# Loading and splitting the input projection's weights ahead of the modulation's weights

## The chip, the cores and the metric

The kernel runs on one core of one Trainium2 chip. The metric is the device time of one execution in microseconds. The core has a matrix engine (TensorE, PE in the profile; its weight loads are PEld), a vector engine (VectorE, DVE), an activation engine (ScalarE, ACT), a general engine (GpSimd, POOL), a queue engine that issues most of the transfers (SyncE, SP), and 16 DMA engines.

## The reference, cut to what matters

One transformer layer over 2048 latent tokens and 256 context tokens of width 1024, all in float32:

```
mod = silu(cond) @ w_ada + b_ada            # 1024 -> 6 x 1024: shift, scale, gate, shift, scale, gate
p   = (layer_norm(x) * (1 + scale) + shift) @ w_in    # 1024 -> 1184: 384 query, 256 key/value, 32 rope, 512 S5
```

`p` feeds a latent attention and a state-space (S5) mixer, whose outputs are projected, added and normalised, and a gated feed-forward block follows. The change touches only the start: the first two of the six parts of `mod` (shift and scale), for latent and context conditions, and the weights `w_in` of the input projection.

## The kernel before

Float32 products are made of three products of rounded halves. `hi_of` (line 53, on GpSimd) rounds a raw tile to its upper half, `lo_of` (line 58, on VectorE) subtracts that from the raw tile, and `mm3` (lines 63 to 65) multiplies high by high, high by low and low by high. The whole program is a chain of stages whose TensorE work is written out one behind the other; the stage around the change is `phase_in`, which takes about the first 390 us.

`phase_in` stages all its loads through one tag, `st`, of a pool with six buffers of 128x1024. In code order it issues:

1. the S5 tables' small loads (`s5_prep`, on ScalarE's queue) and their first transposes,
2. `load(0)`: two tiles of context tokens (`xt`, line 130), and their normalisation (lines 71 to 91 and 137). They keep two of the six buffers until `front(0)` has transposed them,
3. `wada`: sixteen tiles of 512 KB of `w_ada` (line 148), each of which TensorE multiplies by the two conditions straight from the buffer, with four matmul instructions in the trace (line 150), into four PSUM tiles `pa`,
4. `wraw`: sixteen tiles of 296 KB of `w_in` (line 159), each split by GpSimd into `wih` and by VectorE into `wil`, which stay for the whole stage,
5. `mrow`, `pm`, `mod`: the sums are copied (167), transposed (169) and biased (172, 173),
6. `front(0)`: the context tokens are transposed (191, `pt`), modulated (195, `ur`) and split into `uh` and `ul`,
7. the rest of the S5 tables' preparation: exponentials, sine and powers on VectorE (536 to 605), transposes on TensorE (636 `pbt`, 643 `pct`), and products on VectorE (657 to 662). Its scratch `sp_a` and `sp_b` lies in one of the two `uh` and one of the two `ul` buffers,
8. for each of nine groups of 256 tokens: `front` of the next group, `project` of this one (`pkv`, from the second group on `pq`, and `p` for the S5 part), and beside them pieces of two generators, `multiply` and `contract` of the S5 tables (681 to 714, GpSimd products, then `pin` on TensorE and stores from SP's queue) and `modulations` (309 to 323, the other four parts of `mod`, loaded by SP as `wad` and summed on VectorE).

A scheduler orders the instructions of each engine at build time by readiness and by code order. So an engine's order can differ from the code's (VectorE's exponentials of step 7 run in the first 30 us), and then it is fixed: each engine, SP's queue too, takes its instructions in that order. The PSUM tag `tr` has two buffers, which `pm`, `pt`, `pbt` and `pct` take in code order.

Of the kernel before, what the change touches and what calls it, by code (L numbers as in the profile page):

```python
# [10 lines left out]
F32 = mybir.dt.float32  # L11
# [39 lines left out]
def hi_of(eng, hi, raw):  # L51

    eng.tensor_scalar(hi, raw, 1.0, 0.0, ALU.mult, ALU.add)  # L53


def lo_of(eng, lo, raw, hi):

    eng.tensor_tensor(lo, raw, hi.bitcast(F32), ALU.subtract)  # L58
# [39 lines left out]
def phase_in(tc, E):  # L98
    nc = tc.nc
    I = E.I  # L100
    with ExitStack() as st:
        cp = st.enter_context(tc.tile_pool(name="in_c", bufs=1, reuse_waits="tile"))
        stage = st.enter_context(tc.tile_pool(name="in_stage", bufs=6, reuse_waits="tile"))
# [4 lines left out]
        ps_p = st.enter_context(tc.tile_pool(name="in_pp", bufs=1, space=PSUM, reuse_waits="tile"))  # L108
# [12 lines left out]
        cT = cp.tile([128, 32], F32, name="cT")  # L121
        nc.vector.tensor_copy(cT, pc[:, 0, 0:32])

        def load(gi):
            src = I["ctx"][0] if gi == 0 else I["x"][0]
            base = 0 if gi == 0 else (gi - 1) * 256
            xs = []
            for i in range(2):
                x = stage.tile([128, 1024], F32, name="xt", tag="st")
                nc.sync.dma_start(x, src[base + i * 128: base + (i + 1) * 128, :])  # L130
                xs.append(x)
            return xs

        def norm(xs):
            for x in xs:
                mv, rs = ln_stats(nc, sm, x, eps)
                nc.vector.tensor_scalar(x, x, mv[:, 0:1], rs, ALU.subtract, ALU.mult)
            return xs
# [2 lines left out]
        prep = s5_prep(tc, E, cp, tp, stage, up, ps_t, ps_p)  # L141
        next(prep)
        ns0 = norm(load(0))
        pa = [ps_p.tile([2, 512], F32, name="pa%d" % i, tag=t) for i, t in enumerate(("pq", "pkv0", "pkv1", "ps0"))]
        for k in range(8):
            for b in range(2):
                w = stage.tile([128, 1024], F32, name="wada", tag="st")
                nc.sync.dma_start(w, I["w_ada"][0, k * 128:(k + 1) * 128, b * 1024:(b + 1) * 1024])
                for hf in range(2):
                    nc.tensor.matmul(pa[b * 2 + hf], cT[:, k:16:8], w[:, hf * 512:(hf + 1) * 512],  # L150
                                     start=(k == 0), stop=(k == 7))

        whi, wlo = [], []
        for k in range(8):
            hi = wp.tile([128, 1184], F32R, name="wih%d" % k)
            lo = wp.tile([128, 1184], F32R, name="wil%d" % k)
            for o in (0, 592):
                raw = stage.tile([128, 1024], F32, name="wraw", tag="st")
                nc.sync.dma_start(raw[:, 0:592], I["w_in"][0, k * 128:(k + 1) * 128, o:o + 592])
                hi_of(nc.gpsimd, hi[:, o:o + 592], raw[:, 0:592])  # L160
                lo_of(nc.vector, lo[:, o:o + 592], raw[:, 0:592], hi[:, o:o + 592])
            whi.append(hi)
            wlo.append(lo)
        pm = ps_t.tile([128, 16, 2], F32, name="pm", tag="tr")
        for b in range(4):
            mrow = tp.tile([128, 2, 256], F32, name="mrow", tag="ur").rearrange("p a b -> p (a b)")[0:2]
# [1750 lines left out]
def build(tc, ins, out, dbg=None, phases="abcdefg"):  # L1917
# [4 lines left out]
    with ExitStack() as st:  # L1922
# [10 lines left out]
        if "a" in phases:  # L1933
            phase_in(tc, E)
# [72 lines left out]
```

## Time and profile before

| what | us |
|---|---|
| median of three runs | 3241.45 (3236.36 to 3243.56) |
| profiled execution, its own time | 3237.78 |
| its span | 3235.9 |
| TensorE busy | 3064.9 (95%) |
| VectorE, GpSimd, ScalarE busy | 2260.4, 1573.3, 1275.6 |
| DMA, mean over the span | 118 GB/s |

Busy shares are averages over stages with different limits. In a row of the timeline the first number is the start and the second the length in us, and the bracket at the end gives the idle time of the engine before it and what ended it. An engine's name with a q is its instruction queue.

### The profile page before, as it was taken

Reading aid. Unit: us, or ns where it says so; the run is one execution under the profiler, and the core shown is the slowest. Engines: PE = TensorE matmul, PEld = TensorE weight load, DVE = VectorE, ACT = ScalarE, POOL = GpSimd, SP = SyncE. Lnnn points to the kernel's source line nnn. Section 1 sums busy time; section 2 is a strip of 40 time slices with the busy share of each in tenths; the row PEclk is TensorE's granted clock in tenths of the full one; section 3 lists DMA queues with packets and bytes.
Section 4 is the critical chain, followed back from the end, with each engine's and each line's share of the span. In section 5 each row is a group of like instructions: output and inputs, shape, how many; then the busy total and the mean of one; then the engine's idle time right before and its main releaser. Section 6 shows DMA issues by size and latency. Waiting matters only on the chain. (4 is left out here: it accounts for less than half of the span.)

```text
span 3235.9 us, 48094 instructions
## 1 busy us (share of the span) xinstructions
PE 3064.9 (95%) x16693; PEld 2602.4 (80%) x16693; DVE 2260.4 (70%) x3906; ACT 1275.6 (39%) x2400; POOL 1573.3 (49%) x2365
## 2 busy tenths in 40 slices
PE   7899988999999999999888989999999999999998
PEld 3788876989889898889666767888688888888886
DVE  7755356888888776788568586766866666566667
ACT  2333354677777666677635232321300002112110
POOL 3755333777877899935234243332222222243345
PEclk9999999999999999999989999999999999999999
DMA  7454474011111122221677633332422224555544
GB/s 235 156 163 137 131 257 143 25 28 32 33 26 28 51 75 81 77 68 41 158 207 211 183 114 101 121 105 91 147 91 85 85 85 152 190 187 164 176 147 137
DMA packets 372565, 382.14 MB, mean 118 GB/s; under 512 B 97177, under 2 KB 270297, under 8 KB 372321
## 3 DMA queue, kind: packets, MB, share of 16 engines
q1 hardware_dynamic: 302320, 307.31, 31.9%
q10 hardware_dynamic: 70000, 71.75, 6.5%
q8 instruction: 132, 2.16, 0.3%
q14 instruction: 113, 0.92, 0.1%
HBM read 274.48 MB, written 104.48 MB: 117 GB/s over the span
## 5 line engine op out<-in xcount | busy, mean ns | idle before, releaser
L1033 DVE TENSOR_TENSOR ptl<-tps,pth 128x512 fp32r<-128x512 f32 x576 | 380.7, 685 | 99.4 <-ACT pth L1027 99.1
L1027 ACT CAST pth<-tps 128x512 fp32r<-128x512 f32 x576 | 336.0, 586 | 159.3 <-PE tps L1022 144.3
L53 POOL TENSOR_SCALAR gh<-wraw 128x512 fp32r<-128x512 f32 x220 | 179.8, 819 | 423.1 <-PE pc L64 75.3
L1045 PE MATMUL O<-pth,vhl 128*128 128x256 f32 x1152 | 323.3, 304 | 0.6 <-DVE oo L1054 0.6
L1046 PE MATMUL O<-ptl,vhl 128*128 128x256 f32 x1152 | 298.1, 283 | 2.0 <-DVE ptl L1033 1.9
L999 DVE TENSOR_REDUCE mx<-SB 128x1 f32<-128x1280 f32 x128 | 190.7, 1490 | 77.7 <-PE SB L65 77.7
L1046 PEld LDWEIGHTS O<-ptl,vhl 128*128 128x128 f32 x1152 | 219.5, 191 | 10.1 <-DVE ptl L1033 3.5
L1045 PEld LDWEIGHTS O<-pth,vhl 128*128 128x128 f32 x1152 | 218.0, 189 | 7.6 <-ACT pth L1027 1.1
L58 DVE TENSOR_TENSOR gl<-wraw,gh 128x512 fp32r<-128x512 f32 x216 | 166.0, 773 | 79.6 <-POOL gh L53 75.3
L1564 ACT CAST oh<-uraw 128x512 fp32r<-128x512 f32 x144 | 85.5, 620 | 308.5 <-PE pd L64 147.2
L1022 PE MATMUL tps<-ident,PB 128*128 128x128 f32 x1280 | 193.0, 273 | 3.2 <-DVE ptl L1033 3.2
L1010 ACT ACTIVATE PB<-SB,nm 128x1280 f32<-128x1280 f32 x128 | 170.7, 1334 | 4.6 <-DVE nm L1004 4.5
L1022 PEld LDWEIGHTS tps<-ident,PB 128*128 128x128 f32 x1280 | 152.6, 140 | 22.8 <-DVE ptl L1033 6.1
L999 DVE TENSOR_REDUCE mx<-SA 128x1 f32<-128x1024 f32 x128 | 156.0, 1219 | 17.3 <-PE SA L65 17.1
L1022 PE MATMUL tps<-ident,PA 128*128 128x128 f32 x1024 | 152.7, 274 | 1.6 <-DVE ptl L1033 1.6
L58 DVE TENSOR_TENSOR ol<-uraw,oh 128x512 fp32r<-128x512 f32 x136 | 104.6, 790 | 63.0 <-ACT oh L1564 62.8
L63 PE MATMUL SB<-kh,qh 96*128 96x512 f32 (+1 forms) x384 | 145.8, 380 | 0.0
L1010 ACT ACTIVATE PA<-SA,nm 128x1024 f32<-128x1024 f32 x128 | 143.4, 1121 | 5.2 <-DVE nm L1004 5.2
L774 POOL TENSOR_TENSOR sct<-scan_tab,hist 128x128 f32<-128x128 f32 x286 | 132.3, 463 | 24.5 <-ACT hist L763 4.9
L1692 ACT ACTIVATE s<-s 128x512 f32<-128x512 f32 x43 | 27.1, 631 | 286.1 <-DVE s L1691 286.0
L64 PE MATMUL SB<-kl,qh 96*128 96x512 f32 (+1 forms) x384 | 138.3, 360 | 0.0
L65 PE MATMUL SB<-kh,ql 96*128 96x512 f32 (+1 forms) x384 | 138.1, 360 | 0.0
(577 smaller groups left out, 9653.2 us busy)
## 6 DMA issues: line engine op xcount, KB each, us to landing
wraw<-in_w_down SPq DMA_DIRECT2D x198, 256.0 KB
wraw<-in_w_gate_up SPq DMA_DIRECT2D x176, 256.0 KB
h_scr<-s ACTq DMA_DIRECT2D x88, 256.0 KB
uraw<-h_scr SPq DMA_DIRECT2D x88, 256.0 KB
wad<-in_w_ada SPq DMA_DIRECT2D x32, 512.0 KB
wada<-in_w_ada SPq DMA_DIRECT2D x16, 512.0 KB
xt<-in_x SPq DMA_DIRECT2D x16, 512.0 KB
att_scr<-oo SPq DMA_DIRECT2D x64, 128.0 KB
```

The source lines that it names most:

```text
L53: eng.tensor_scalar(hi, raw, 1.0, 0.0, ALU.mult, ALU.add)
L58: eng.tensor_tensor(lo, raw, hi.bitcast(F32), ALU.subtract)
L63: nc.tensor.matmul(out, sh, mh, start=first, stop=False, skip_group_check=onto)
L64: nc.tensor.matmul(out, sh, ml, start=False, stop=False, skip_group_check=onto)
L65: return nc.tensor.matmul(out, sl, mh, start=False, stop=last, skip_group_check=onto)
L999: nc.vector.reduce_max(mx, SB if u else SA, axis=AX.X)
L1010: nc.scalar.activation(ex, SB if u else SA, AF.Exp, bias=hd.nm[:, u, t:t + 1], scale=SCALE, accum_out=hd.sums[:, u, t:t + 1])
L1022: nc.tensor.transpose(ps[:, kk, j * 128:(j + 1) * 128], pr.P[(j, u)][:, o:o + 128], ident)
L1027: nc.scalar.copy(hi, pr.pt[g][0])
L1033: nc.vector.tensor_tensor(lo, ps, hi.bitcast(F32), ALU.subtract)
L1045: nc.tensor.matmul(o, vk, hi[:, kk, :], start=k in (0, 8), stop=False)
L1046: nc.tensor.matmul(o, vk, lo[:, kk, :], start=False, stop=k in (7, 17))
```

## The change

The block that loads `w_ada` and multiplies it moves behind the block that loads and splits `w_in`. No instruction is added or removed, and no shape changes. SP's queue gets the sixteen `wraw` loads ahead of the sixteen `wada` loads; GpSimd's and VectorE's splits come ahead of TensorE's sixty-four `wada` matmuls in code order.

```diff
         ns0 = norm(load(0))
-        pa = [ps_p.tile([2, 512], F32, name="pa%d" % i, tag=t) for i, t in enumerate(("pq", "pkv0", "pkv1", "ps0"))]
-        for k in range(8):
-            for b in range(2):
-                w = stage.tile([128, 1024], F32, name="wada", tag="st")
-                nc.sync.dma_start(w, I["w_ada"][0, k * 128:(k + 1) * 128, b * 1024:(b + 1) * 1024])
-                for hf in range(2):
-                    nc.tensor.matmul(pa[b * 2 + hf], cT[:, k:16:8], w[:, hf * 512:(hf + 1) * 512],
-                                     start=(k == 0), stop=(k == 7))
 
         whi, wlo = [], []
         for k in range(8):
...
                 lo_of(nc.vector, lo[:, o:o + 592], raw[:, 0:592], hi[:, o:o + 592])
             whi.append(hi)
             wlo.append(lo)
+        pa = [ps_p.tile([2, 512], F32, name="pa%d" % i, tag=t) for i, t in enumerate(("pq", "pkv0", "pkv1", "ps0"))]
+        for k in range(8):
+            for b in range(2):
+                w = stage.tile([128, 1024], F32, name="wada", tag="st")
+                nc.sync.dma_start(w, I["w_ada"][0, k * 128:(k + 1) * 128, b * 1024:(b + 1) * 1024])
+                for hf in range(2):
+                    nc.tensor.matmul(pa[b * 2 + hf], cT[:, k:16:8], w[:, hf * 512:(hf + 1) * 512],
+                                     start=(k == 0), stop=(k == 7))
         pm = ps_t.tile([128, 16, 2], F32, name="pm", tag="tr")
```

## Rows read from the trace of the kernel before

**Rows 1.** The page: busy time of TensorE, and the chain that ended last.
```profile
PE 3064.9 (95%) x16693; PEld 2602.4 (80%) x16693; DVE 2260.4 (70%) x3906; ACT 1275.6 (39%) x2400; POOL 1573.3 (49%) x2365
...
PE 34%; DVE 3%; issue 1%; POOL 1%; DMA 1%; ACT 0%; SPq 0%; DVEq 0%; POOLq 0%; ACTq 0%
```

**Rows 2.** Stretches: length, busy us (instructions) by engine, PEclk, DMA share, GB/s.
```profile
0.00:10.00 10.00, 0.60 (x3) 0.38 (x3) 6.26 (x36) 1.59 (x2) 0.70 (x6) 1.00 0.65 208
10.00:30.00 20.00, 19.05 (x37) 3.11 (x37) 18.88 (x122) 3.26 (x6) 0.00 (x0) 1.00 1.03 303
30.00:42.90 12.90, 12.48 (x29) 2.18 (x29) 0.34 (x1) 1.15 (x2) 1.01 (x2) 1.00 0.82 266
42.90:45.20 2.30, 1.94 (x21) 1.59 (x20) 1.47 (x4) 1.05 (x2) 2.17 (x2) 1.00 0.38 103
45.20:110.00 64.80, 48.91 (x314) 41.67 (x314) 57.99 (x97) 25.30 (x59) 54.20 (x58) 0.89 0.59 182
110.00:400.00 290.00, 271.20 (x1901) 248.62 (x1902) 156.91 (x480) 109.63 (x325) 150.17 (x195) 0.98 0.45 142
```

**Rows 3.** Weight tiles: instructions, duration ns min/median/max, first and last start us.
```profile
L150 PE MATMUL pa<-wada,cT x64: 592/592/1057, 10.3 to 42.3; 128*2 128x512 f32 x64
L159 SPq DMA_DIRECT2D wraw<-in_w_in x16: 327/328/423, 37.2 to 58.7; - x16
L53 POOL TENSOR_SCALAR wih<-wraw x16: 678/1194/1307, 41.8 to 67.9; 128x592 fp32r<-128x592 f32 x16
L58 DVE TENSOR_TENSOR wil<-wraw,wih x16: 776/1208/1270, 42.6 to 68.7; 128x592 fp32r<-128x592 f32 x16
```

**Rows 4.** TensorE waits for the rest of the stretch 45 to 110: us, times, longest.
```profile
PE pkv L64 <- DVE wil L58: 4.5, 3, 1.8
PE pq L63 <- POOL uh L53: 3.4, 2, 3.2
PE pkv L63 <- POOL wih L53: 2.5, 2, 1.8
PE pt L191 <- DVE xt L137: 2.4, 2, 1.3
```

**Rows 5.** Timeline of SP's queue, first seven loads of the modulation's weights.
```profile
4.24 2.01 SPq L148 DMA_DIRECT2D wada<-in_w_ada  x3
...
13.70 5.17 SPq L148 DMA_DIRECT2D wada<-in_w_ada  x4
```

**Rows 6.** What SP's queue waited for, 3 to 30 us: us, times, longest.
```profile
SPq L148 <- PE pa L150: 12.0, 8, 2.2
SPq L148 <- DMA sp_d<-in_s_c_re: 7.4, 1, 7.4
```

**Rows 7.** Timeline: the sixth load's issue, and its first use.
```profile
16.83 0.33 SPq L148 DMA_DIRECT2D wada<-in_w_ada  x1
...
20.83 0.09 PEld L150 LDWEIGHTS pa<-wada,cT 128*2 128x2 f32 x2 [0.83 <-DMA wada<-in_w_ada]
```

**Rows 8.** Timeline of TensorE: first and last modulation matmuls, then the first projection.
```profile
10.29 8.22 PE L150 MATMUL pa<-wada,cT 128*2 128x512 f32 x12
...
41.48 1.45 PE L150 MATMUL pa<-wada,cT 128*2 128x512 f32 x3
...
47.46 0.40 PE L63 MATMUL pkv<-wih,uh 128*128 128x288 f32 x1 [0.45 <-POOL uh L53]
47.70 0.30 PE L64 MATMUL pkv<-wil,uh 128*128 128x288 f32 x1
```

**Rows 9.** Timeline of VectorE: the modulation is ready; the S5 tables' last product.
```profile
45.01 0.16 DVE L173 SCALAR_TENSOR_TENSOR mod<-pm,cT 128x16 f32<-128x16 f32 x1
...
77.58 1.22 DVE L662 TENSOR_TENSOR sp_x<-sp_b 64x1024 f32<-64x1024 f32 x1
```

**Rows 10.** Timeline of GpSimd: the first product that needs those tables.
```profile
78.88 1.26 POOL L681 TENSOR_TENSOR w<-sp_x,sp_t 128x256 f32<-128x256 f32 x2 [6.66 <-DVE sp_x L662]
```

**Rows 11.** TensorE's longest waits, 110 to 400 us: us, times, longest.
```profile
PE pq L292 <- ACT kvc L276: 13.0, 6, 4.9
```

**Rows 12.** Timeline around one of them: SP's queue, then VectorE.
```profile
149.72 0.33 SPq L696 DMA_DIRECT2D out_scr<-yt  x1
150.15 0.37 SPq L130 DMA_DIRECT2D xt<-in_x  x1
...
157.90 1.29 DVE L89 BATCH_NORM_STATS2 bst<-xt 128x6 f32<-128x512 f32 x2 [2.13 <-DMA xt<-in_x]
```

## The prediction

> **What bounds the kernel now.** I read the page first: TensorE is busy for 95% of the span, and the chain that ended last lies mostly on it [rows 1]. So what counts is when TensorE has its operands, and a time lost or won at the start is passed on to the end unless a later stage gives it back. Next I cut the first 400 us into stretches [rows 2]. The reader should see three regimes. From 10 to 43 us TensorE is nearly full, with the modulation's matmuls alone, and the DMA engines move 266 to 303 GB/s; GpSimd has nothing to do and VectorE runs the tables' arithmetic until 30 us. From 45.2 to 110 us, when the projections begin, TensorE is busy for only 48.91 of 64.80 us at a mean clock of 0.89, while VectorE (57.99) and GpSimd (54.20) are almost full. From 110 us on TensorE is busy for 271.2 of 290. The third view, the waits of that middle stretch, says why it is bad: TensorE waits for `wil` and `wih`, the splits of the projection's weights, for the normalised tokens and for their halves, all from the two overloaded engines [rows 4]. The splits run from 41.8 to 69.9 us, sixteen of 1.19 us on GpSimd and sixteen of 1.21 us on VectorE [rows 3].
>
> **What the change moves.** It takes the splits out of the bad stretch and puts them into the time when GpSimd idles. In exchange the modulation, which every projection needs through `front(0)`, is loaded 4.85 MB later (16 tiles of 128x592 floats). Both sides have to be priced.
>
> *The price: the modulation is late.* SP's queue now starts with the `wraw` loads. Before, three loads were issued by 6.25 us and the fourth at 13.70 [rows 5], held for 7.4 us by the landing of an S5 table load, `sp_d` [rows 6], which goes by the load's place in the queue and so holds the fourth `wraw` load now. Three loads of 303 kB instead of 524 kB leave 0.66 MB less in flight, 2.2 us at the 303 GB/s of [rows 2]; so the fourth load goes between 11.5 and 13.7, and I take 12.6. From there the buffers, four free ones out of six as before, set the pace. The nearest row is the same sixteen loads through the same buffers: 37.2 to 58.7 us, 1.44 us apiece [rows 3], with `front(0)`'s splits in between. Thirteen such intervals bring the first `wada` load to 31.3. Bounds: 1.00 us apiece if only DMA limits (303 kB at 303 GB/s), from 11.5, gives 24.5; if VectorE first clears all of its 18.88 us of tables' work from 10 us on [rows 2] and thirteen splits of 1.21, it gives 44.6.
>
> From issue to first use a load took 4.0 us [rows 7], so TensorE starts at 35.3. Its modulation matmuls took from 10.29 to 42.93, 32.6 us [rows 8], and I keep that: it holds a slow start (the first twelve took 8.22 us, against 592 ns pipelined for the rest [rows 3, 8]), and TensorE comes from a rest in both kernels. They end at 67.9. The copies, transposes and bias take from 42.93 to 45.17 [rows 8, 9], 2.2 us. The modulation is ready at 70.1 instead of 45.2: 24.9 us later. With the two bounds it is 63.3 or 83.4.
>
> The Trainium skill's page "TensorE: Matmul & The Clock Gate", section Part 1 on the HAM clock gate, says that a rested TensorE starts at half rate and is let up only by sustained activity. The first matmuls at 1057 ns against 592 [rows 3] agree with it. By that rule the gap between the last modulation matmul and the first projection would bring a second slow start; it is a rival below.
>
> *The gain: the stretch behind the modulation has no splits in it.* Of the 64.80 us from 45.2 to 110, 15.9 are TensorE's idle time, and 11% of its 48.91 busy ones, 5.4, are lost to the lower clock that the granted clock of 0.89 shows: 21.3 us together [rows 2]. The same work takes 43.5 us if nothing is late. What stays: about 1 us until `front(0)` hands over its first halves (the first projection came 2.3 us after the modulation, with transposes in between [rows 8, 9]), and the ordinary small waits, which were 18.8 us in the 290 after 110, less the 13.0 of one particular wait [rows 2, 11]: 2%, or 0.9 us. So 19.4 us are won.
>
> *Edits costed at nothing.* The number of instructions, bytes and loads is the same. GpSimd's splits cost nothing early, since GpSimd is idle until 41.84. VectorE's cost nothing as long as the exponentials, sine and powers that they push back are done before `pbt` is ready, which is behind `front(0)` in the PSUM tag's order and hence behind 70 us: 18.9 + 19.3 us of work from 10 us on end at 48.2. The token loads `xt` stay behind both sets of weights, as before. The tables' transposes and products (636 to 662) cannot go ahead of `front(0)`, so they move back with the modulation; they were done 33.6 us behind it [rows 9], beside the splits, and now have VectorE for themselves while TensorE has the first group's projection to do.
>
> *The sum.* 24.9 later, 19.4 won: 5.5 us slower, that is 3237.78 + 5.5 = 3243.3. By the bounds the modulation's 63.3 gives 1.3 us faster (18.1 against 19.4) and its 83.4 gives 18.8 slower. The profiled execution lies 3.7 us below the median of the three runs and inside their spread; against the median the same sum is 3247. What a measurement of this kernel can tell from no change is 0.2%, 6.5 us. So the likeliest result is a change within that bound, on the slow side: the stretch only exchanges one idle time of TensorE (splits late) for another (modulation late).
>
> **The rivals.**
>
> *The early splits are slow (slower).* VectorE is at 94% from 10 to 30 us [rows 2], its order is fixed at build time, and a buffer is free only when VectorE has made its `wil`. If tables' work stands between two splits, the interval grows from 1.44 us, and each 0.1 us costs 1.3. From 1.52 us on the result is slower by over 6.5. At 2.2 us apiece, half way to the upper bound, it is 5.5 + 9.9 = 15.4 slower: 3253. For it speaks the busy share; against it that the tables' operations are short (122 in 20 us) and that code order puts the splits ahead. Chance 0.25. The Trainium skill, page "SBUF — State Buffer", section "Who interferes with whom", states that GpSimd and a VectorE operation with two SBUF inputs lock each other out of a shared port; the split's 678 ns at least and 1194 at the median [rows 3] agree, and by it the tables' two-input operations would stretch too.
>
> *The tables are late (slower).* The `uh` buffer of the second group is held by the tables' scratch. If their chain behind `front(0)` takes as long as before, GpSimd stands as it did for 6.66 us [rows 10] and the second `front` comes after TensorE has run out of the first group: 5.5 + 6.7, 3250. It decides when the last product comes over 28 us behind the modulation. Against it: half of the 33.6 us before were spent beside splits. Chance 0.09.
>
> *A second slow start (slower).* At the modulation TensorE has some 4.5 us with only small transposes. At half rate for the 5.9 us that the first slow start lasted it would lose 3: 8.5 slower, 3246. But the same lull stood before the first projection of the kernel before, with a granted clock of 1.00, and the projections then came 0.13 to 0.24 us apart [rows 2, 8]. Chance 0.04.
>
> *The later waits vanish (faster).* From 110 us on TensorE waits 13.0 us in six pieces for `kvc` [rows 11]. Behind the longest is VectorE, held by an `xt` tile, whose load stood in SP's queue behind the store of a table that GpSimd had late [rows 12]. With no splits behind the modulation GpSimd may be in time. If all 13.0 go, the result is 7.5 faster: 3230. It decides only if nearly all go, and GpSimd's tables also start later than before. Chance 0.14.
>
> *The order on the engines barely changes,* because the scheduler moves work as it likes: SP's order followed the code in the weight loads [rows 3, 5], so 0.03, and it falls to no change.
>
> **How the numbers follow.** Within 0.2%: 0.45 for the sum and 0.03 for no effect, 0.48. Slower: 0.25 + 0.09 + 0.04 = 0.38. Faster: 0.14. The predicted time is the sum, 3243. The range reaches from 3233, below the early bound by half the way to the faster rival, to 3255, which takes in the three slower ones and most of the late bound. The likeliest case's own range is 3236 to 3248.
>
> **What would show it.** The first `wada` load near 31 us (24 to 45), `mod` near 70 (63 to 83), `wih` and `wil` done by 35 to 48, TensorE idle from 10 to 35; behind `mod` no wait for `wil` or `wih`, and about 44 us of nearly full TensorE until the same work is done as at 110 before, so near 115. If `mod` comes earlier than 62, or the 13.0 us of `kvc` waits shrink, I am wrong on the fast side; if the loads of `w_in` are over 1.5 us apart, or TensorE stands before the second group's `pq`, on the slow side.

## The result, and the profile after

The kernel after takes 3265.26 us (median of four runs, 3263.24 to 3267.66), the kernel before 3240.86 in the same measurement (3236.36 to 3243.56). The ratio is 1.0073 [1.0057, 1.0089]: 24.4 us or 0.75% slower. The predicted 3243 and its range to 3255 were too fast.

The profiled execution has a span of 3262.3 us instead of 3235.9, with TensorE as busy as before [rows 1]:

```profile
PE 3061.7 (94%) x16693; PEld 2603.8 (80%) x16693; DVE 2256.4 (69%) x3906; ACT 1276.5 (39%) x2400; POOL 1571.9 (48%) x2365
```

To find where the time was lost I look for a product late enough to have passed the whole input stage and early enough to be clear of the feed-forward part. The attention's products `O` (line 1045) serve: these are the rows by tile of the kernel before and then of the kernel after, with count, duration in ns and the first and the last start.

```profile
L1045 PE MATMUL O<-pth,vhl x1152: 278/283/562, 574.7 to 1561.7; 128*128 128x256 f32 x192
```
```profile
L1045 PE MATMUL O<-pth,vhl x1152: 278/283/382, 597.2 to 1584.0; 128*128 128x256 f32 x192
```

The first comes 22.5 us later and the last 22.3: all of this is lost ahead of 597 us, and nothing in the next 987 us gives it back. I call it the lag; it is taken for every kernel below. The rest of the 26.4 us between the two spans, some 4, comes behind the last of these products. Nothing is read from it: whole executions of the kernel before differ among themselves by more than that (3237 to 3253 on one chip).

Now the start, by the same stretches as in [rows 2]: the early rest, the modulation's matmuls, the hand-over, the stretch that answers to 45.2 to 110, and the 289.8 us behind it.

```profile
10.00:30.00 20.00, 0.37 (x1) 0.18 (x1) 16.09 (x38) 2.97 (x4) 9.89 (x12) 1.00 0.82 212
34.00:68.30 34.30, 30.12 (x65) 5.37 (x65) 17.25 (x94) 2.59 (x5) 1.70 (x2) 1.00 0.84 274
68.30:72.40 4.10, 2.03 (x21) 1.61 (x20) 3.92 (x16) 1.59 (x5) 0.00 (x0) 1.00 0.78 269
72.40:132.20 59.80, 43.54 (x310) 38.54 (x311) 43.80 (x83) 27.36 (x64) 43.87 (x49) 0.88 0.34 107
132.20:422.00 289.80, 273.56 (x1907) 251.30 (x1906) 149.72 (x467) 106.30 (x319) 143.54 (x190) 0.97 0.44 140
```

The weight tiles, against [rows 3]: loads of `w_in` first, splits done at 37.7, modulation matmuls from 37.8 to 68.3.

```profile
L162 PE MATMUL pa<-wada,cT x64: 592/592/1057, 37.8 to 67.8; 128*2 128x512 f32 x64
L160 SPq DMA_DIRECT2D wada<-in_w_ada x16: 327/328/328, 34.0 to 61.2; - x16
L151 SPq DMA_DIRECT2D wraw<-in_w_in x16: 327/328/684, 4.2 to 31.5; - x16
L53 POOL TENSOR_SCALAR wih<-wraw x16: 679/801/1223, 11.0 to 34.6; 128x592 fp32r<-128x592 f32 x16
L58 DVE TENSOR_TENSOR wil<-wraw,wih x16: 705/770/1247, 11.7 to 36.9; 128x592 fp32r<-128x592 f32 x16
```

So the loads and the modulation came where they were forecast. The stretch behind them did not. It has about the work of before's 64.80 us (310 matmuls in place of 314; 18 fewer of `pkv` and 14 more transposes of tokens) and takes 59.80, of which TensorE stands for 16.3 and loses 12% of 43.54, 5.2, to the lower clock: 21.5, as much as the 21.3 that were to go. TensorE's waits there, against [rows 4]:

```profile
PE pq L63 <- ACT qn L219: 6.9, 1, 6.9
PE pin L701 <- POOL w L683: 6.3, 1, 6.3
PE pt L191 <- DVE rq_o L80: 1.4, 1, 1.4
PE pin L701 <- DVE kpad L713: 1.2, 1, 1.2
```

No wait for `wil` or `wih` is left. In their place stand two of over 6 us that before did not have. The first, on TensorE's timeline:

```profile
93.91 0.28 PE L64 MATMUL p<-ul,wih 128*128 128x256 f32 x1
100.48 0.69 PE L701 MATMUL pin<-ident,w 128*128 128x128 f32 x2 [6.28 <-POOL w L683]
101.09 1.03 PE L704 MATMUL pin<-yt,sp_x 128*16 128x128 f32 x4
102.06 0.58 PE L65 MATMUL p<-uh,wil 128*128 128x256 f32 x1
102.44 0.41 PE L63 MATMUL p<-uh,wih 128*128 128x256 f32 x1
```

The `pin` transposes, a piece of the S5 tables that the first group's calls of `beside` bring, stand in TensorE's order between two matmuls of one projection. The projection's next matmul (line 65) needs nothing new, and still waits 6.28 us for a product `w` of another chain. That product, on GpSimd, follows from the tables' last product on VectorE (compare [rows 9, 10]):

```profile
72.26 0.17 DVE L173 SCALAR_TENSOR_TENSOR mod<-pm,cT 128x16 f32<-128x16 f32 x1
...
92.73 1.61 DVE L662 TENSOR_TENSOR sp_x<-sp_b 64x1024 f32<-64x1024 f32 x1
...
121.15 1.53 DVE L313 SCALAR_TENSOR_TENSOR acc<-wad,cT,acc 128x1024 f32<-128x1024 f32 x1 [6.97 <-DMA wad<-in_w_ada]
```
```profile
85.08 3.14 POOL L688 TENSOR_TENSOR yt<-sp_y,sp_t 128x288 f32<-128x288 f32 x2 [6.66 <-ACT sp_y L650]
96.90 2.12 POOL L681 TENSOR_TENSOR w<-sp_x,sp_t 128x256 f32<-128x256 f32 x2
99.70 0.72 POOL L683 TENSOR_TENSOR w<-w,w 128x256 f32<-128x256 f32 x1
```

The last row of VectorE's timeline is behind the second wait. VectorE stands 6.97 us for `wad`, a load of the other modulation parts. The splits `ul` of the next tokens stand behind it, ScalarE's `ur` waits for their buffers, and the work for `qn` stands behind `ur` in ScalarE's order:

```profile
125.56 1.93 ACT L195 ACTIVATE ur<-pt,mod 128x256 f32<-128x256 f32 x4 [8.76 <-DVE ul L58]
```

In SP's queue that load was issued right behind a store of the same late tables, which waited for GpSimd's `yt` and had held the queue since 108.66. These are SP's waits in the first 110 us, and its timeline where the load goes:

```profile
SPq L696 <- POOL yt L690: 20.0, 3, 11.1
SPq L151 <- DMA sp_d<-in_s_c_re: 4.6, 1, 4.6
```
```profile
108.29 0.37 SPq L698 DMA_DIRECT2D k_scr<-kpad  x1
115.46 0.32 SPq L696 DMA_DIRECT2D out_scr<-yt  x1
115.88 0.37 SPq L309 DMA_DIRECT2D wad<-in_w_ada  x1
```

**The theory** from this: the modulation is late by what was priced. It does not come back because the S5 tables are late with it: their pieces stand in the fixed orders of TensorE and of SP's queue among the first group's work, and block work that is ready. **The rivals:** the late stores alone do it, through SP's queue; the tables are held back by the PSUM tag that they share with `front`; or the lateness of the modulation alone does it, whatever becomes of the tables.

### The profile page after: what moved, and what is told of

It is laid out like the page before. It is cut to its first block, busy times and chain, and to the rows that moved or that the text cites. A ratio compares the mean times of both kernels' runs of the same rounds, so it can differ in the third digit from the quotient of the medians.

```text
span 3262.3 us, 48105 instructions
## 1 busy us (share of the span) xinstructions
PE 3061.7 (94%) x16693; PEld 2603.8 (80%) x16693; DVE 2256.4 (69%) x3906; ACT 1276.5 (39%) x2400; POOL 1571.9 (48%) x2365
```

## The experiments

The lag is measured from the first and last starts of the two rows above, one profiled execution each; the other kernels' starts come from the same row of their traces. Ratios are to the kernel before on the same chip. A lag has some noise: kernels with the same code up to the modulation have it ready at 71.4 to 72.4 us (four of them ordered as after) and at 45.2 and 46.7 (before, and before with its pieces shifted), so differences of 1 to 2 us between lags are not read.

| kernel | first and last `O`, us | lag, us | time, us | ratio |
|---|---|---|---|---|
| after | 597.2, 1584.0 | 22.5, 22.3 | 3265.26 | 1.0073 [1.0057, 1.0089] |
| after, tables first | 581.3, 1568.4 | 6.6, 6.7 | 3254.18 | 1.0023 [1.0009, 1.0037] |
| before, tables first | 572.4, 1558.7 | -2.3, -3.0 | 3241.64 | 0.9986 [0.9975, 0.9997] |
| after, stores from GpSimd | 593.9, 1581.3 | 19.2, 19.6 | 3267.04 | one run |
| after, half the modulation | 575.7, 1561.3 | 1.0, -0.4 | 3243.94 | one run |
| after, no pieces in the first group | 587.7, 1575.8 | 13.0, 14.1 | 3259.53 | one run |
| after, tables in another PSUM tag | 598.3, 1585.7 | 23.6, 24.0 | 3266.18 | 1.0064 [1.0049, 1.0079] |
| before, halves on ScalarE | 571.8, 1559.2 | -2.9, -2.5 | 3244.64 | 0.9996 [0.9987, 1.0006] |
| before, tables in another PSUM tag | 577.1, 1563.6 | 2.4, 1.9 | 3247.49 | 1.0003 [0.9993, 1.0012] |
| after, pieces shifted | 587.2, 1572.9 | 12.5, 11.2 | 3256.66 | 1.0035 [1.0021, 1.0050] |
| before, pieces shifted | 575.1, 1562.0 | 0.4, 0.3 | 3241.52 | 0.9994 [0.9983, 1.0005] |
| before, halves on ScalarE, pieces shifted | 566.0, 1553.0 | -8.7, -8.7 | 3239.33 | 0.9979 [0.9969, 0.9990] |
| before, halves on ScalarE, tables first | 567.4, 1555.6 | -7.3, -6.1 | 3238.70 | 0.9976 [0.9967, 0.9985] |

**Tables first, in after and in before.** The rest of the tables' preparation (lines 536 to 662) goes ahead of the `wada` block.

```diff
             wlo.append(lo)
+        next(prep)
         pa = [ps_p.tile([2, 512], F32, ...
...
         u = front(0, ns0)
-        next(prep)
```

> The changed kernel with one more move: the rest of the S5 tables' preparation (636 to 662) is issued behind the splits and ahead of the modulation's loads, so that its transposes come ahead of the modulation's tile in the PSUM tag. Theory A (the tables' chain paces the stretch behind the modulation: they could only start behind it, GpSimd's products start behind them): the last product comes before 60 us instead of 94, TensorE's waits of 6.3 us at 100 and 6.9 us at 131 go, and some 15 to 20 us come back: 3245 to 3251. Rival B (only the modulation's 27 us count, and the work behind it takes as long as ever): it stays at 3262 to 3268.

Measured: the lag falls from 22.4 to 6.6 us, though the modulation itself comes 3.2 us later still, at 75.6. The last table product and the first `w` are at:

```profile
50.00 1.22 DVE L662 TENSOR_TENSOR sp_x<-sp_b 64x1024 f32<-64x1024 f32 x1
```
```profile
58.99 0.75 POOL L683 TENSOR_TENSOR w<-w,w 128x256 f32<-128x256 f32 x1
```

The first of the 6 us waits is gone. Of the second 3.0 us are left, and it ends at 117.05; ahead of it TensorE's longest wait from 75.6 us on is 1.6 for `uh`. Here the stretch up to 116.3, which takes in most of that wait, is near what the prediction wanted: 40.7 us at a clock of 0.96, though for 254 matmuls, since the tables' 48 transposes have gone ahead of it:

```profile
75.60:116.30 40.70, 35.35 (x254) 33.04 (x254) 35.27 (x82) 17.40 (x49) 25.59 (x32) 0.96 0.49 154
```
```profile
PE pkv L63 <- POOL uh L53: 1.6, 1, 1.6
```
```profile
117.05 0.46 PE L63 MATMUL pq<-wih,uh 128*128 128x384 f32 x1 [2.96 <-ACT qn L220]
```

So 15.8 of the 22.4 us hang on the place of the tables, and the rival of the modulation's lateness alone falls as the whole cause.

> The kernel before (modulation's loads first) with the same move: the tables' preparation ahead of the modulation's loads. Theory A: the tables are done in the hole that VectorE has from 30 to 42 us, GpSimd's products start right behind the splits, and the stretch from 45 to 110 us loses 5 to 10 of its 21 lost us: 3231 to 3236. Rival B: the modulation comes at 45 as before and nothing changes, 3241.

Measured: the same move is worth only 2.3 to 3.0 us in the kernel before, where the modulation then comes at 52.0 instead of 45.2; 4.4 of these 6.8 us are the tables' transposes, which stand in TensorE's order among the modulation's matmuls. The tables are a burden that the change made, not one that both kernels bear alike.

**Stores from GpSimd's queue.** In after:

```diff
-        nc.sync.dma_start(E.out_scr[:, g], yt[:, GC:GC + 2 * CH * GC])
+        nc.gpsimd.dma_start(E.out_scr[:, g], yt[:, GC:GC + 2 * CH * GC])
```

and the same for the two `nc.sync.dma_start(*stored.pop())`.

> The changed kernel with the S5 tables' stores issued from GpSimd's queue instead of SP's. Theory C (SP's queue, held by stores whose tables are late, keeps token and modulation loads back, and that is what stretches the time behind the modulation): the 7 us wait of VectorE at 121 goes and 6 to 12 us come back: 3253 to 3259. Theory A: the products themselves are late, so at most 3 us: 3262 or more, since GpSimd has to issue the stores as well.

Measured: the lag falls by 3, and TensorE keeps both waits, as its waits of 70 to 140 us show.

```profile
PE pin L701 <- POOL w L683: 8.0, 1, 8.0
PE pq L63 <- ACT qn L219: 6.6, 1, 6.6
```

Theory C was right that VectorE's wait for `wad` goes, but not that this frees TensorE. VectorE now stands for the next tokens' halves, which GpSimd makes behind the tables' products and stores in its own order (its waits from 105 to 135 us):

```profile
DVE ul L58 <- POOL uh L53: 8.2, 4, 5.5
```

So SP's queue alone is not the cause: with it free, GpSimd's order does nearly the same.

**Half the modulation.** In after, `for k in range(8)` becomes `range(4)` (with the matmul's stop at `k == 3`): half of the modulation's sum is left out.

> The changed kernel with half of the modulation's sixteen loads and matmuls left out (half of the sum is missing). The modulation then comes some 14 us earlier, at 58. Theories A and B: everything behind it hangs on it, so the whole kernel comes 12 to 15 us earlier, 3250 to 3253. Rival D (the loss is fixed by the new order on the engines, whatever the modulation does): it stays within 5 us of 3265.

Measured: the modulation comes 16.4 us earlier, at 56.0, and the lag falls by 21.5 and 22.7, to about zero. The waits move with it, unchanged in length (TensorE's, 50 to 120 us):

```profile
PE pq L63 <- ACT qn L219: 7.0, 1, 7.0
PE pin L701 <- POOL w L683: 6.3, 1, 6.3
```

So the whole of it, tables included, is tied to the modulation's time, as steps 6 and 7 of the code order say. That the lag fell by 5 to 6 more than the modulation moved is not explained.

**No pieces in the first group.** In after, `beside` asks the tables' generator only from the second group on:

```diff
-            next(prep, None)
+            if gi:
+                next(prep, None)
```

> The changed kernel, but the pieces of the S5 table generator are not called beside the first group's projections, only from the second group on (the rest at the end, as the code allows). Theory A1 (the late products hurt because TensorE's order has their `pin` in front of ready projections: 6.3 us at 100, and what follows at 131): these waits go and 8 to 14 us come back of the 22 that the attention stage starts late: attention 8 to 14 us late. Theory A2 (the tables' chain hurts because its scratch holds the second group's `uh` buffer, so the second group is late whatever the pieces do): under 4 us come back.

Measured: TensorE waits 2.2 us at most in 43 to 160, both 6 us waits are gone, and the lag is 13.0, though the last table product is still at 93.4.

```profile
PE p L63 <- ACT s5p L258: 2.2, 1, 2.2
PE pt L191 <- DVE xt L137: 1.9, 2, 1.5
```

The lag was 6.1 after the fourth group and grew to 13 at the end of the stage, where the pieces left over run. To see if only that end was at fault, the pieces were dealt out instead.

**Pieces shifted, in after and in before.** None in the first group, four extra ones later:

```diff
         def beside(gi):
-            next(prep, None)
+            calls[0] += 1
+            if gi:
+                next(prep, None)
+            if calls[0] in (10, 14, 18, 22):
+                next(prep, None)
```

> The changed kernel with no table pieces beside the first group's projections, and the four left out made up by one extra piece in each of the groups 2 to 5, so that none is left for the end. Theory A1 (TensorE's order has late table pieces among ready projections): the first groups' loss of about 14 us comes back as in the run without pieces, and the 7 us that the leftover pieces cost at the end of the stage go as well: the attention is 6 to 8 us late, 3247 to 3254. Rival (the leftover pieces were not what cost the 7 us): attention 12 to 14 us late, 3255 to 3262.

> The kernel before with the same shift of the table pieces. There TensorE waited only 0.6 us for a table product, so by theory A1 little is to be had: 0 to 4 us earlier, 3240 to 3246. Rival (pieces beside the first group cost as much in any order of the loads): 10 us or more earlier, 3235 or less.

Measured: the lag is 12.5 and 11.2 in after and 0.4 in before. That the leftovers were the cost falls: dealt out, the lag grew as well, from 7.8 after the third group to 13.8 after the seventh. The lags at the last `p` product of a group, and at the first `O`, show where the time goes:

| lag, us | modulation | group 1 | group 2 | group 3 | first `O` |
|---|---|---|---|---|---|
| after | 27.3 | 28.4 | 23.0 | 20.5 | 22.5 |
| after, no pieces in the first group | 26.4 | 22.4 | 9.1 | 6.1 | 13.0 |
| after, pieces shifted | 26.2 | 22.5 | 9.0 | 7.8 | 12.5 |
| after, tables first | 30.5 | 17.6 | 8.8 | 6.4 | 6.6 |
| before, pieces shifted | 1.5 | -0.8 | -4.7 | -4.2 | 0.4 |

In before the shift wins 4.7 us by the end of the second group and gives them back: four pieces keep TensorE busy for some 3.7 us wherever they stand (0.92 us each, from 112.75 to 113.67 us in after). In after it wins 14.0 by then and keeps 10: there the pieces in the first group cost not only their own time, but that of the waits for them.

**The tables' PSUM tag, in after and in before.** The prediction said that the tables cannot go ahead of `front(0)` because of the tag's order. The tag is changed:

```diff
-            pt = ps_t.tile([128, 512], F32, name="pbt", tag="tr")
+            pt = ps_p.tile([128, 512], F32, name="pbt", tag="sp")
```

and the same for `pct`.

> The changed kernel with the code order as it is, but the tables' transposes (`pbt`, `pct`) take the PSUM buffer of `pin` instead of the tag `tr`, where they stand behind the modulation's tile. If this order in the tag is what ties the tables to the modulation, the scheduler moves them into TensorE's rest from 10 to 35 us, the last product is done by 60, and the time is that of the run with the tables ahead: attention about 7 us late, 3247 to 3254. If the code order alone decides, they stay behind the modulation: 3262 to 3268.

> The kernel before with the tables' transposes in the PSUM buffer of `pin`. Theory A: they leave the stretch behind the modulation for the time ahead of it, at the price of TensorE's time between the modulation's matmuls; the last product comes before 60 us instead of 78.8, and 2 to 6 us are won, 3235 to 3241. Rival: what TensorE gives them ahead of the modulation delays that by as much, no change.

Measured: nothing is won in either. In after only the first `pbt` moved (to 18.2 us); ScalarE's copy of it still stands behind `front(0)`:

```profile
66.02 0.57 ACT L167 COPY mrow<-pa 2x512 f32<-2x512 f32 x1 [27.29 <-PE pa L162]
...
72.74 2.06 ACT L195 ACTIVATE ur<-pt,mod 128x256 f32<-128x256 f32 x4 [1.14 <-DVE rq_o L80]
74.69 0.57 ACT L637 COPY sp_b<-pbt 64x512 f32<-64x512 f32 x1
```

ScalarE was free for the 27 us before, so the tag is not what holds the copy; its place in ScalarE's order is. Why the scheduler puts it there was not tried.

**Versions of before.** If the splits in the stretch were the fault of before, there is a way to relieve it without delaying the modulation: the upper halves are rounded by ScalarE, which is idle there.

```diff
-                hi_of(nc.gpsimd, hi[:, o:o + 592], raw[:, 0:592])
+                nc.scalar.copy(hi[:, o:o + 592], raw[:, 0:592])
```

> The kernel before, with the upper halves of the projection's weights made by ScalarE instead of GpSimd. It takes the sixteen operations from GpSimd in the stretch from 42 to 68 us, and the splits on VectorE no longer run beside them. If the splits bound that stretch (theory A of the gain: 21 lost us there), the last `wil` comes some 5 us earlier and 4 to 8 us are won: 3233 to 3237. If ScalarE's share of the tables and of `front` is delayed as much, no change: 3241 to 3245.

> The kernel before with the upper halves of the projection's weights made by ScalarE and the table pieces shifted: a try to beat both. If GpSimd's and VectorE's load from 42 to 100 us is what holds TensorE, attention starts 5 to 9 us earlier: ratio 0.997 to 0.9985. If the loads of the weights bound it by now, under 3 us: 0.999 to 1.000.

> The kernel before with the tables' preparation ahead of the modulation's loads and the upper halves on ScalarE: the other try. The tables ahead gave 3 us, the halves 2.5; if they add up, attention comes 5 to 6 us earlier, ratio 0.998. If the tables' copies and the halves are in each other's way on ScalarE, nothing is won over either: 0.999 to 1.000.

Measured: alone it is worth 2.9 us of lag, within what the total can show. With the pieces shifted it is worth 8.7, with the tables first 6 to 7, and both beat the two kernels: 0.9979 and 0.9976. The shift alone gained nothing in before and tables first 3: it is when the splits no longer make TensorE wait that the pieces of the tables cost something there as well. With the halves on ScalarE alone, TensorE's waits of 45 to 110 us have none left for `wih` or `wil`, and the wait for the first piece has grown from 0.6 to 4.9 us:

```profile
PE pin L701 <- POOL w L683: 4.9, 1, 4.9
```

That is the same exchange as in after. Part of the 8.7 may be noise: the modulation is ready at 44.0 there and at 46.5 with the halves alone.

## Why the prediction was wrong

*The price was nearly right.* The fourth `wraw` load went early, at about 7.8 us; the landing of the S5 load held the fifth until 12.85 (4.6 us above). The twelve intervals from there to the first `wada` at 34.0 took 1.76 us apiece, against 1.44 forecast. So the rival of slow early splits did reach its point, 1.52, but with one load fewer to pace, and with matmuls that took 30.5 instead of 32.6 us it made the last of them end at 68.3 for 67.9; that these errors cancel is luck. The hand-over took 4.1 us instead of 2.2: VectorE was busy for 3.92 of 4.10 us there, with the next tokens' normalisation among `mod`'s steps. The modulation was ready at 72.4 for 70.1, 27.2 us later instead of 24.9. That is 2.3 us of the miss.

*The failed step is "the stretch behind the modulation has no splits in it".* It took the idle time of before's stretch to come from the splits, directly or by the load that they put on two engines, and gave back 19.4 of the 21.3 us when they were gone. 5.0 were won, 64.80 less 59.80: 27.2 - 5.0 = 22.2, the lag. The splits did go, and so did their waits. But the next wait in line was not looked for: the sum asked only what is removed, not what comes second.

*The edit costed at nothing that was not nothing is the tables.* "They move back with the modulation" was right; that they "now have VectorE for themselves" too: they were done 21.9 us behind the modulation (94.3), not 33.6, well under the 28 us from which the rival of late tables was to decide. It was the place that was wrong. The rival priced the buffer that their scratch holds for the second group; what bound were the `pin` pieces in TensorE's order within the first group, and GpSimd's late products, which held the second group through the stores in SP's queue or, with those moved, through GpSimd's own order. The pins' product `w` came at 100.4, by which time TensorE had run everything ahead of it.

The 22.4 us by the runs: 15.8 go when the tables are ahead of the modulation. There the modulation came 3.2 us later, so the stretch behind it won 19.0. Of those, 10 to 11 are the waits for late pieces in the first group (shifted, they leave a lag of 12.5 and 11.2). Some 5 may be the tables' 48 transposes: they hold TensorE behind the modulation in six bursts of 0.63 to 1.19 us, 4.9 together, between the matmuls of `pkv` from 77.3 to 83.6, where before had them in a stretch that waited for splits anyway; with the tables first they run in TensorE's rest:

```profile
16.08 3.62 PE L636 MATMUL pbt<-ident,sp_d 64*64 64x64 f32 x32 [5.89 <-DMA sp_d<-in_s_b_re]
19.63 3.21 PE L643 MATMUL pct<-ident,sp_d 128*64 128x128 f32 x16
```

No run moved the transposes alone, so this part is argued; for the last 3 to 4 us there is no reason on record. Both stay open. The remaining 6.6 are near the 5.5 of the sum, but by luck: the modulation was 30.5 us late there, not 24.9, and more than the forecast 19.4 came back, with the help of the transposes.

*The other rivals.* The order on the engines did change. The waits for `kvc` went from 13.0 [rows 11] to 10.9 in the 289.8 us behind, far from vanishing. The second slow start, given 0.04, is there but small: granted clock 0.78 from 72.4 to 80.0 (row below), a loss of 22% of 7.08 busy, 1.6 us. The sign that the prediction named for the slow side, TensorE standing before the second group's `pq`, is the wait of 6.9 us.

```profile
72.40:80.00 7.60, 7.08 (x53) 6.32 (x53) 6.72 (x15) 4.98 (x10) 3.05 (x4) 0.78 0.39 123
```

The Trainium skill's page "PSUM — Partial Sum Buffer", section "Engine vs sequencer instructions", says that matmuls start and complete in program order and that the queues of ScalarE, VectorE and GpSimd are strictly first in, first out. The 6.28 us of a ready projection behind `pin` agree, and by that rule the prediction should have read TensorE's order in the first group, not only its operands. SP's queue, which that sentence does not name, stood 11.1 us behind one store here.

## What to carry to other kernels

When a wait is removed, look on the same engine for the instruction that waits next: an idle time is the latest of several waits, and the others hide behind it. When a producer is moved back, follow everything that code order puts behind it, and find the places where its consumers stand in other engines' fixed orders in front of ready work; here those places, not the buffers, set the price. Relieving the crowded stretch in place (halves on the idle engine, side work dealt out later) gained 0.2%, where moving its work ahead of the chain that starts everything lost 0.75%.

## What the hardware showed that was not expected

A long wait of TensorE costs more than its length. Behind the 6.28 us, the projections follow each other 0.21 us apart (102.44, 102.65, 102.86, 103.08 on the timeline) instead of 0.12 (93.44, 93.56, 93.67, 93.79), nearly the whole ratio of the two clock levels, 1.2 and 2.4 GHz. By stretches:

```profile
80.00:90.00 10.00, 9.75 (x76) 8.51 (x77) 9.63 (x8) 9.24 (x18) 4.84 (x4) 1.00 0.40 120
90.00:100.00 10.00, 4.19 (x36) 3.98 (x34) 8.11 (x16) 3.73 (x9) 9.69 (x10) 0.84 0.60 189
98.00:100.00 2.00, 0.00 (x0) 0.00 (x0) 2.00 (x9) 1.88 (x5) 1.92 (x3) 0.50 0.97 365
100.00:110.00 10.00, 8.75 (x53) 7.31 (x54) 6.91 (x21) 2.56 (x11) 9.84 (x13) 0.81 0.24 90
110.00:120.00 10.00, 9.70 (x72) 9.04 (x71) 4.17 (x9) 3.19 (x8) 9.69 (x12) 1.00 0.37 109
```

While TensorE waits, the granted clock falls to 0.50, 1.2 GHz, and after the wait that ends at 100.48 it is 0.81 on average for 8.75 busy us: 1.7 us more. A stretch can print 1.00 for want of a record: the clock's record starts at 42.3 us (in before at 16.2), just where the modulation's matmuls go from 1057 to 592 ns, so the 1.00 from 34 us (in [rows 2] from 10 us) says nothing of those ahead of it. Also, the same 32 splits took 801 and 770 ns at the median where GpSimd was busy for 9.89 of 20 us, instead of 1194 and 1208 [rows 3] where both engines were almost full; no run tells why.
